# Preparing three output tiles inside the attention stage, in memory that the pooled weights leave

## The chip, the core and the metric

The kernel runs on one core of one Trainium2 chip. The core has a matrix engine (TensorE, in the profile PE, its weight loads PEld), a vector engine (DVE), a scalar engine (ACT), a general engine (POOL) and a queue that issues most transfers (SP). The metric is device microseconds of one execution; a time is the median of several executions.

## The reference

A two-layer encoder trunk is applied with the same weights to two inputs: `x_prompt` (2048 tokens of 1024 numbers) and `x_sample` (512 tokens). One layer is

```
h    = rms_norm(x, pre_g)
u, zp, q, k, v, za = split(h @ w_in)                  # 1024 -> 3072
pool = pooling_mixer(u) * silu(zp)                    # 4 windows, a small map per group
q, k = rope(q), rope(k)                               # 4 heads, 2 maps each, 64 wide
o    = (softmax(q0 k0) - lam * softmax(q1 k1)) @ v    # per head, v 128 wide
attn = rms_norm(o, subln_g) * (1 - lambda_init) * silu(za)
y    = concat(pool, attn) @ w_out                     # 1024 -> 1024
x    = x + rms_norm(y, post_g)
```

All arrays are float32.

## The kernel before

Every product is made of three matrix products of numbers split in a high and a low part (fp32r), so that almost every tensor that TensorE reads has first been through `split`: a copy of the high part, mostly on ACT, and a subtraction for the low part, on DVE or POOL. PSUM has eight banks of 128 x 512: four called `sc`, two `tr`, one `ot`, one `mm`. A name's banks are used in turn, so a new user of a bank waits for the last reader of its old contents.

**Order.** The instructions of PE, ACT, DVE and POOL run in the order in which the Python code issues them (`manual_schedule`). SP is not in that set: its transfers are put in order by the compiler's own schedule, by when their data and memory are expected to be free. Memory is taken from two stacks of pools, one growing from the left and one from the right; a pool that is opened where a closed one lay makes each of its tiles wait for the old tiles under it.

**Attention** (`attention`). Work comes in blocks of one head and 256 queries. A block of the prompt has four lots, a block of the sample has one; a lot is four score tiles of 128 x 512. In one pass of the loop, called a step here, PE computes the scores of a lot (L441, L442), ACT takes the exponentials of the lot before (L468), DVE the maxima of the present one (L452, L448), PE turns two units of older probabilities by transposes (`flip`, L493) into a `tr` bank, which ACT and DVE split (L110, L115), and multiplies units by the values (`values`, L510). The score of a lot goes into the `sc` bank that the exponential of the lot before has to read first. When a block's exponentials are done, POOL joins its two maps (`combine`, L474 to L484); only then can the block be turned. `finish` and `scales` (L515 to L550) square the result, multiply by `sg` and the gate, store it to `mh` in DRAM (L521) and compute each token's and head's scale, kept in `rstat`.

**The filler.** TensorE has other work to fill each step with: `fill` takes six matmuls per step, first of the input projections that are left and then of `pooled_outputs` (L699), the pooled half of the output projection, whose results go through bank `mm` and tile `yo` to `ys` in DRAM. The weights of this half lie in pool `wop` (eight tiles of 4 KB per partition), those of the attention half in `woa`. With them lie, on the right, `yo`, `mixp` (pooled inputs) and `kv` (keys and values of the sample) in the stack `aux`, and one raw weight row `wor` in `kept`.

**The end of attention.** The last block of the prompt's head 3 is followed by the last one of the sample. When the latter's lot is made, `mix_ahead` asks for the first 256 tokens of `mh` in the `wor` tile (L1088). Once no lot is left, each step also takes ten pieces of `first_outputs` (L1091): for the first two token tiles (128 tokens each), `spread` puts each token's scale into a row by four transposes (L744, into a `tr` bank), `rescale` multiplies (L748, DVE) and splits (ACT high, POOL low, tile `mixp`), and then come the 48 matmuls (L754) of the two tiles with the attention half of `w_out`, into the four `sc` banks.

In what follows the steps of the end are named by what PE does in them. Step A holds the last prompt lot, step B the sample's last lot, step C no lot and the last six matmuls of the pooled outputs; D to H turn the last prompt block and the last sample block, two units each, and the attention ends after H.

**The output stage** (`phase3`). For each of the 20 token tiles: load `y` (the pooled half) and `mixh` (the attention output, for two tiles at once); `scale`, that is `spread` and `rescale`, two tiles ahead; 24 matmuls (`products`); `y = ps + y` on DVE (L800); then `post`: square sum on ACT (L839), its power on POOL (L843), product on DVE (L845), sum with the residual `xr` on POOL (L847), store. Its pools `y`, `d`, `m` are opened on the left after attention's. In layer 0 the next layer's pools (86 KB) are opened below them, and from the thirteenth tile on `nxt.prepare` adds the norms and transposes (L172, L177, in `tr` banks) of layer 1.

## Time and profile before

| | us |
|---|---|
| median of 3 runs | 3176.3 (3175.72 to 3178.85) |
| the profiled execution | 3172.6 |
| its span | 3170.6 |
| PE busy | 3070.9 |
| DVE, ACT, POOL busy | 2057.8, 1719.0, 1773.2 |

The profiled execution lies 3.7 us below the median, and 2.0 us of it lie outside the span. A line of a timeline gives start, duration, engine, source line, operation and how often, and in brackets the idle time before it and what ended it. A line of the waits gives the sum, the count and the longest of one kind of wait. A table of stretches gives, for each, its length, the busy time of each engine with instructions in brackets, the clock that TensorE was granted (1.00 is full) and the DMA share. The profile says 0.99 for the clock over the whole span.

### The profile page before, as it was taken

The numbers are of one execution on the slowest core, as the hardware profiler recorded it, in microseconds if no ns is written. First come the engines' busy times: TensorE is split into PE (matmuls) and PEld (weight loads), VectorE is DVE, ScalarE is ACT, GpSimd is POOL, SyncE is SP. The second block draws the span as 40 slices with busy tenths as digits, with TensorE's granted clock in tenths as the row PEclk, the third lists the DMA queues.
The fourth block names the chain that finished last, engine by engine and source line by source line (L and its number), as shares of the span: only waits on it lengthen the run. The fifth ranks groups of instructions, "written<-read, shape, count | busy, mean of one in ns | idle before, by whom it ended". The sixth has DMA issues, their size and how long they took to land. (4 is left out here: it accounts for less than half of the span.)

```text
span 3170.6 us, 48480 instructions
## 1 busy us (share of the span) xinstructions
PE 3070.9 (97%) x17016; PEld 2590.7 (82%) x17016; DVE 2057.8 (65%) x3249; ACT 1719.0 (54%) x3915; POOL 1773.2 (56%) x1978
## 2 busy tenths in 40 slices
PE   8999999999999999998999999999999999999888
PEld 6898888778887888886778888887788878888776
DVE  3354255688888887774634543556888988777644
ACT  3244233377777777772332442333777777777622
POOL 1000122289997888885710001122999978888846
PEclk9999999999999999998999999999999999999999
DMA  5354357643424334435854544577434243353367
GB/s 200 117 159 148 125 159 206 205 139 94 130 67 137 104 107 141 125 98 194 317 174 120 157 140 132 171 200 222 117 91 124 64 140 114 97 152 114 91 212 260
DMA packets 298900, 464.54 MB, mean 147 GB/s; under 512 B 26144, under 2 KB 180768, under 8 KB 298656
## 3 DMA queue, kind: packets, MB, share of 16 engines
q1 hardware_dynamic: 292032, 439.42, 46.3%
q10 hardware_dynamic: 6624, 22.02, 1.8%
q8 instruction: 134, 2.20, 0.3%
q14 instruction: 110, 0.90, 0.1%
HBM read 293.57 MB, written 167.77 MB: 146 GB/s over the span
## 5 line engine op out<-in xcount | busy, mean ns | idle before, releaser
L452 DVE TENSOR_REDUCE mx<-sc 128x1 f32<-128x512 f32 x1024 | 649.9, 683 | 184.8 <-PE sc L442 184.6
L468 ACT ACTIVATE e<-sc,nm 128x512 f32<-128x512 f32 x1088 | 732.4, 694 | 32.0 <-DVE nm L455 28.4
L484 POOL TENSOR_TENSOR e<-e,e 128x1024 f32<-128x1024 f32 (+1 forms) x288 | 666.5, 2314 | 24.0
L278 PE MATMUL sc<-hth,wh 128*128 128x512 f32 x1408 | 555.7, 395 | 0.0
L278 PE MATMUL sc<-htl,wh 128*128 128x512 f32 x1408 | 554.4, 394 | 0.0
L278 PE MATMUL sc<-hth,wl 128*128 128x512 f32 x1408 | 552.7, 393 | 0.7 <-DVE ss L166 0.7
L110 ACT ACTIVATE ath<-tr 128x512 fp32r<-128x512 f32 x544 | 329.2, 606 | 259.6 <-PE ot L510 190.4
L441 PE MATMUL sc<-ks,q 128*128 128x512 f32 x1024 | 434.8, 425 | 3.4 <-ACT e L468 3.4
L442 PE MATMUL sc<-ks,q 128*128 128x512 f32 x1024 | 406.1, 397 | 0.0
L115 DVE TENSOR_TENSOR atl<-tr,ath 128x512 fp32r<-128x512 f32 x544 | 364.7, 682 | 53.4 <-ACT ath L110 53.3
L510 PE MATMUL ot<-ath,v 128*128 128x256 f32 x2176 | 368.1, 291 | 7.7 <-DVE mt L520 7.7
L493 PEld LDWEIGHTS tr<-ident,e 128*128 128x128 f32 x2176 | 267.3, 141 | 91.5 <-DVE atl L115 22.4
L493 PE MATMUL tr<-ident,e 128*128 128x128 f32 x2176 | 329.6, 275 | 11.8 <-DVE atl L115 9.9
L483 POOL TENSOR_SCALAR e<-e,nco 128x1024 f32<-128x1024 f32 (+1 forms) x288 | 327.8, 1138 | 15.0
L510 PEld LDWEIGHTS ot<-ath,v 128*128 128x128 f32 x2176 | 309.4, 189 | 32.0 <-DVE mt L520 11.1
L168 POOL TENSOR_TENSOR rs<-ss,mhalf 128x1 f32<-128x1 f32 x40 | 25.5, 638 | 554.0 <-DVE ss L166 554.0
L278 PEld LDWEIGHTS sc<-hth,wl 128*128 128x128 f32 x1408 | 264.6, 188 | 60.2 <-DVE wl L115 1.2
L278 PEld LDWEIGHTS sc<-hth,wh 128*128 128x128 f32 x1408 | 264.7, 188 | 58.5 <-POOL wl L115 0.3
L278 PEld LDWEIGHTS sc<-htl,wh 128*128 128x128 f32 x1408 | 264.7, 188 | 57.5 <-DVE htl L115 0.4
L441 PEld LDWEIGHTS sc<-ks,q 128*128 128x128 f32 x1024 | 194.3, 190 | 65.1 <-ACT e L468 38.7
L115 DVE TENSOR_TENSOR wl<-wr,wh 128x1024 fp32r<-128x1024 f32 x94 | 121.3, 1293 | 183.5 <-ACT wh L110 182.0
L468 ACT ACTIVATION_READ_ACCUMULATOR e<-sc,nm 128x1 f32 x1088 | 231.6, 213 | 0.0
(151 smaller groups left out, 5729.5 us busy)
## 6 DMA issues: line engine op xcount, KB each, us to landing
wr<-in_w_in SPq DMA_DIRECT2D x128, 512.0 KB, 4.2
q<-qs_p SPq DMA_DIRECT2D x128, 256.0 KB, 4.1
ks_p<-hl SPq DMA_DIRECT2D x64, 256.0 KB, 3.3
vs_p<-hl SPq DMA_DIRECT2D x128, 128.0 KB, 2.6
qs_p<-hl SPq DMA_DIRECT2D x64, 256.0 KB, 3.5
mp_p<-hl SPq DMA_DIRECT2D x32, 512.0 KB, 3.7
ks<-ks_p SPq DMA_DIRECT2D x64, 256.0 KB, 5.8
v<-vs_p SPq DMA_DIRECT2D x32, 512.0 KB, 6.1
```

Of the source, the lines that this page charges most:

```text
L110: nc.scalar.activation(hi, src, AF.Copy)
L115: lo_eng.tensor_tensor(lo, src, f32(hi), op=ALU.subtract)
L168: nc.gpsimd.tensor_tensor(rs, ss, mhalf[:, :1], op=ALU.pow)
L278: nc.tensor.matmul(ps, lhsT=w[k // 4][m][:, k % 4, ns], rhs=h[:, k, :], start=k + i == 0, stop=k == KT - 1 and i == 2)
L441: nc.tensor.matmul(ps, lhsT=q[:, m, 0, ts], rhs=kk, start=True, stop=False)
L442: nc.tensor.matmul(ps, lhsT=q[:, m, 1, ts], rhs=kk, start=False, stop=True)
L452: nc.vector.reduce_max(s["mx"][:, ch : ch + 1], s["ps"][ch], axis=AX.X)
L468: nc.scalar.activation(dst, s["ps"][ch], AF.Exp, bias=s["nm"], accum_out=s["b"]["z"][s["qt"]][:, m, ch : ch + 1])
L483: nc.gpsimd.tensor_scalar(x1[:, :n], x1[:, :n], nco, 0.0, op0=ALU.mult, op1=ALU.add)
L484: nc.gpsimd.tensor_tensor(x0[:, :n], x0[:, :n], x1[:, :n], op=ALU.add)
L493: nc.tensor.transpose(ps[:, j, qt * P : (qt + 1) * P], e[kt // 8][:, kt % 8 * P : (kt % 8 + 1) * P], ident)
L510: nc.tensor.matmul(b["ot"][:, :QB], lhsT=b["vs"][v][kt // 8][:, kt % 8, :], rhs=at[:, j, :], start=unit + i == 0, stop=kt == nkt - 1 and i ...
```

## The change

`first_outputs` is rewritten, and the memory around it rearranged.

- The first tile is scaled and split one step earlier: when the sample's last lot is made, at the end of step A, `fill.first(1)` runs its `spread` and `rescale`. The product goes to a `yo` tile, the parts to the raw weight tile on the left.
- The rest waits until the filler is empty: `fill_first` returns as long as pooled products or their tails are left. Then `aux` is closed, that is `wop`, `yo` and `mixp`, and the output stage's pools `d` and `m` are opened in that memory. The next 256 tokens of `mh` are asked for, tile 1 is scaled and split, tile 0 multiplied, tile 2 scaled and split, tile 1 multiplied.
- In these three the low parts are subtracted on DVE, not on POOL. In the output stage POOL does it as before.
- `phase3` takes `d` and `m` as they are, with tile 2 ready. Its `spread` writes bank `mm` (the filler's) instead of a `tr` bank. The `scale` of tile 2 there ends at once.
- `kv` moves from `aux` to `kept`, which now stays open to the end of the stage.
- In the last layer a tile of 72 KB is opened below pool `y` and never used, so that `y` lies where attention's `q`, `k`, `e1` and `raw` lay instead of `e0` and `v`.

```diff
+PAD = 18 * 1024
...
+                        if qb == nq - 1:
+                            fill.first(1)
                         yield from block(sa, n // ns, n % ns, *skv)
...
-    def rescale(ps, src, m, hl):
+    def rescale(ps, src, m, hl, lo_eng):
         nc.vector.tensor_tensor(m, ps.rearrange("p (h n) -> p h n", h=H), src, op=ALU.mult)
-        split(hl[:, 0], hl[:, 1], m, nc.scalar, nc.gpsimd)
+        split(hl[:, 0], hl[:, 1], m, nc.scalar, lo_eng)
...
-    def phase3(l, wo, scaling, pairs, early, kept, es, nxt):
+    def phase3(l, wo, scaling, pairs, early, ready, ph, mixed, kept, es, nxt):
+        if not nxt:
+            es.enter_context(sbuf("pad", 1)).tile([P, PAD], F32, name="pad")
         y_p = es.enter_context(sbuf("y", 6))
-        mixed = ExitStack()
-        d_p = mixed.enter_context(sbuf("d", 3))
-        m_p = mixed.enter_context(sbuf("m", 3))
+        d_p, m_p = ph["d"], ph["m"]
...
-            ps = bank("tr")
+            ps = bank("mm")
             spread(ps, s["st"], s["t"])
...
-        for s in tiles[:3]:
+        for s in tiles[:2]:
             for _ in scale(s):
                 pass
...
-            if 3 <= n + 2 < len(order):
+            if n + 2 < len(order):
                 scaling.append(scale(tiles[n + 2]))
-            if n == 2:
-                kept.close()
...
         mixed.close()
+        kept.close()
...
-                po.update(open_pools(kept, "right", wor=1))
-                po.update(open_pools(aux, "right", wop=1, yo=2, mixp=2, kv=1))
+                po.update(open_pools(kept, "right", wor=1, kv=1))
+                po.update(open_pools(aux, "right", wop=1, yo=2, mixp=2))
...
             def first_outputs():
-                split_tiles = []
-                for t in range(2):
+                def prepare(t, m, hl):
                     ps = bank("tr")
                     spread(ps, pr, t)
+                    rescale(ps, pairs["p", t // 2 * 2 * P][:, :, t % 2 * P : (t % 2 + 1) * P], m, hl, nc.vector)
+                    ready["p", t] = hl
                     yield
-                    m = po["yo"].tile([P, TB], F32, name="yo").rearrange("p (h n) -> p h n", h=H)
-                    hl = po["mixp"].tile([P, 2, H, P], F32R, name="mixp")
-                    rescale(ps, pairs["p", 0][:, :, t * P : (t + 1) * P], m, hl)
-                    split_tiles.append(hl)
-                    yield
-                for t, hl in enumerate(split_tiles):
+                def multiply(t):
                     early["p", t] = []
                     for ns in halves:
                         ps = bank("sc")
                         early["p", t].append(ps)
-                        for i, _ in enumerate(head_products(ps, hl, wo, ns)):
+                        for _ in head_products(ps, ready["p", t], wo, ns):
                             yield
+                m = po["yo"].tile([P, TB], F32, name="yo").rearrange("p (h n) -> p h n", h=H)
+                yield from prepare(0, m, pa["raw"].tile([P, 2, H, P], F32R, name="wor"))
+                aux.close()
+                ph["d"] = mixed.enter_context(sbuf("d", 3, "right"))
+                ph["m"] = mixed.enter_context(sbuf("m", 3, "right"))
+                pairs["p", 2 * P] = ph["d"].tile([P, H, 2 * P], F32, name="mixh")
+                nc.sync.dma_start(pairs["p", 2 * P], pr["mh"][:, :, 2 * P : 4 * P])
+                for t in range(2):
+                    yield from prepare(t + 1, ph["m"].tile([P, H, P], F32, name="mixs"), ph["m"].tile([P, 2, H, P], F32R, name="hl"))
+                    yield from multiply(t)
...
             def fill_first(n):
+                if n > 2 and (products or tails or fresh):
+                    return
                 for _ in range(n):
                     next(first, None)
```

## The prediction

> **What bounds the kernel now.** First the page: one engine is busy nearly all the time, so the question is only what PE waits for, where the change works.

> ```profile
> span 3170.6 us, 48480 instructions
> ## 1 busy us (share of the span) xinstructions
> PE 3070.9 (97%) x17016; PEld 2590.7 (82%) x17016; DVE 2057.8 (65%) x3249; ACT 1719.0 (54%) x3915; POOL 1773.2 (56%) x1978
> ```

> Then PE's waits from step B to the first tiles of the output stage, in layer 0 (1416 to 1476 us) and layer 1 (2993 to 3053 us, its three longest):

> ```profile
> PE sc L754 <- POOL mixp L115: 7.4, 1, 7.4
> PE sc L754 <- DVE y L800: 5.9, 1, 5.9
> PE sc L754 <- ACT mixp L110: 1.0, 1, 1.0
> PE tr L532 <- DVE shl L115: 0.9, 1, 0.9
> PE tr L532 <- ACT shl L110: 0.7, 1, 0.7
> PE ot L510 <- DVE mt L520: 0.5, 1, 0.5
> ```

> ```profile
> PE sc L754 <- POOL mixp L115: 7.4, 1, 7.4
> PE sc L754 <- ACT hl L110: 6.9, 1, 6.9
> PE sc L754 <- ACT mixp L110: 1.0, 1, 1.0
> ```

> Two holes in each layer: one in step C, where the early products wait for their low parts, and one where the output stage begins. They cost more than the wait: afterwards PE runs at a lower granted clock. The table of stretches, begun where PE takes up work after each hole, shows it (length, busy time and instructions of PE, PEld, DVE, ACT and POOL, granted clock, DMA share, GB/s):

> ```profile
> 1433.87:1437.49 3.62, 3.62 (x14) 3.04 (x14) 0.00 (x0) 0.80 (x2) 1.18 (x1) 0.53 0.19 72
> 1469.10:1475.02 5.92, 5.92 (x16) 4.66 (x17) 2.43 (x4) 2.93 (x5) 1.81 (x3) 0.52 1.04 399
> 3011.14:3014.60 3.46, 3.46 (x13) 2.87 (x14) 0.00 (x0) 0.73 (x2) 1.18 (x1) 0.56 0.54 173
> 3047.26:3053.15 5.89, 5.33 (x16) 3.91 (x17) 2.34 (x4) 2.93 (x5) 2.29 (x2) 0.62 1.04 388
> 1554.32:1557.60 3.28, 3.28 (x16) 2.56 (x16) 3.27 (x3) 2.44 (x6) 3.28 (x2) 1.00 0.67 184
> 1563.41:1567.36 3.95, 3.95 (x12) 3.29 (x13) 2.48 (x4) 2.06 (x3) 3.23 (x4) 0.55 0.68 188
> ```

> Length times (1 - clock) is the loss: 3.62 x 0.47 = 1.7, 5.92 x 0.48 = 2.8, 3.46 x 0.44 = 1.5, 5.89 x 0.38 = 2.2. So the holes cost 1.0 + 7.4 + 1.7 + 5.9 + 2.8 = 18.8 us in layer 0 and 1.0 + 7.4 + 1.5 + 6.9 + 2.2 = 19.0 in layer 1. Why the first is so long shows on POOL in layer 0:

> ```profile
> 1417.47 0.47 POOL L477 TENSOR_TENSOR zc<-zc 128x4 f32<-128x4 f32 x2 [2.81 <-ACT e L468]
> ...
> 1420.30 2.40 POOL L484 TENSOR_TENSOR e<-e,e 128x1024 f32<-128x1024 f32 x1
> ```

> The low parts (L115) are issued to the same queue behind the joining of the last prompt block and of the sample's. Yet the prompt's first half of keys is joined at 1422.7, and only that is needed for PE's next transposes.

> **The change part by part.** *Removed.* Step C no longer scales, splits and multiplies; PE goes straight to step D. The work itself (two spreads, 48 products) is only moved, and a third spread comes forward from the output stage: PE's sum of work is the same. Gone are the waits of 1.0 and 7.4 and the slow clock behind them: 10.1 in layer 0, 9.9 in layer 1. The ten products per step, held back by one step, now also lie in step G (ten instead of two), ahead of the values that waited 0.5 for `mt`: that goes too, in each layer.

> *Tile 0 ahead of step B.* Its input is there: the transfer into `wor` was issued early, since SP's order is not the program's.

> ```profile
> L1088 SPq DMA_DIRECT2D wor<-mh_p x2: 534/534/535, 1246.1 to 2823.4; - x2
> ```

> But its high part stands in ACT's queue ahead of the exponentials of the last prompt lot, and the scores of step B reuse the banks that these read. Before, ACT began them at 1414.61 and PE the scores at 1416.26:

> ```profile
> 1414.61 0.68 ACT L468 ACTIVATE e<-sc,nm 128x512 f32<-128x512 f32 x1
> ```
> ```profile
> 1416.26 0.40 PE L441 MATMUL sc<-k,q 128*128 128x512 f32 x1
> ...
> 1423.88 1.03 PE L744 MATMUL tr<-ident,rstat_p 128*128 128x128 f32 x8
> ```
> ```profile
> L110 ACT ACTIVATE ath<-tr 128x512 fp32r<-128x512 f32 x544 | 329.2, 606 | 259.6 <-PE ot L510 190.4
> ...
> L115 DVE TENSOR_TENSOR atl<-tr,ath 128x512 fp32r<-128x512 f32 x544 | 364.7, 682 | 53.4 <-ACT ath L110 53.3
> ```

> Now: spread 0.6 from 1416.26, product 0.68, copy 0.61, so the first exponential starts at 1418.2 (3.6 later than before) and ends at 1418.9. PE, free at 1416.6 after its four transposes, waits 2.3; with the later banks I take 2.4 per layer. The ends are 0 and the whole 3.6. The joining on POOL moves by the same 3.6: it starts at 1421.1, and the first half is ready 5.2 later (as from 1417.47 to 1422.7), at 1426.3. PE, which came to its spreads of step C at 1423.88, comes to the transposes of step D 0.4 + 2.4 later than that, at 1426.7. That it still has to wait for POOL is just avoided, by 0.4 us.

> *Tile 1 in step D.* Its spread follows both groups of transposes and takes the bank of the first, which ACT and DVE must first split: 0.61 + 0.68 = 1.3 us of new wait per layer (0 to 2). Tile 2, in step E or F, stands behind values and five products and waits for nothing; its `mixh` is asked for three steps ahead. The two subtractions of the tail on DVE have two inputs in SBUF. The nearest such instruction beside a working POOL is this:

> ```profile
> L845 DVE SCALAR_TENSOR_TENSOR y<-y,ry,gpost x39: 1268/1285/2317, 1476.8 to 3158.6; 128x1024 f32<-128x1024 f32 x39
> ```

> It takes 1.3, at worst 2.3. Only tile 1's subtraction falls into POOL's joining (of the sample); I take half of that extra 1.0, rounded up to 0.6, per layer, with 0 and 1.3 as ends. [...]

> *The output stage's start.* Tile 2 is ready, so the 6.9 for `hl` in layer 1 goes. In layer 0 the hole was DVE's sum, whose `y` came late:

> ```profile
> 1461.18 0.33 SPq L521 DMA_DIRECT2D mh_s<-mt  x1
> 1461.56 0.43 SPq L764 DMA_DIRECT2D gpost<-in_post_norm_g  x1
> 1462.05 2.43 SPq L771 DMA_DIRECT2D y<-ys_p  x4
> ```

> The `y` loads stood in SP's queue behind the last store of attention. I read the queue as placing them when all the memory under pool `y` is free: before, that included `kv` and `mixp` (layer 0) and `e0` (layer 1), used to the end. After it, in both layers the last user is tile 0's `hl` in the raw tile, done in step E, some 15 us earlier, while the DMA engines are nearly idle. So `y` is there. What is late next is DVE: after the last scales (two instructions of 256 columns, about 0.5 each) comes the sum that frees a bank, 0.68: 1.7 us of wait, near the hole of 2.1 in the 1554 row after which the clock stayed at 1.00, so no slow clock. The pad, `kv`'s move and `kept`'s later end add no instruction.

> *Bank `mm`.* In layer 0, while the next norm is prepared, PE waits for DVE, which lags with the rescaling:

> ```profile
> PE tr L177 <- DVE mixs L748: 7.8, 2, 5.7
> ```
> ```profile
> 1545.33 0.60 PE L744 MATMUL tr<-ident,rstat_s 128*128 128x128 f32 x4
> ...
> 1551.59 0.60 PE L744 MATMUL tr<-ident,rstat_s 128*128 128x128 f32 x4
> ...
> 1554.32 0.66 PE L177 MATMUL tr<-ident,xt 128*128 128x128 f32 x4 [2.13 <-DVE mixs L748]
> ```
> ```profile
> 1562.59 0.68 DVE L748 TENSOR_TENSOR mixs<-tr,mixh 128x512 f32<-128x512 f32 x1
> ```

> With the spreads in a bank of their own the transposes L177 wait no more, but each spread waits for the rescaling of the tile before: the one at 1551.59 until 1554.3 (2.7), the next, due at about 1561.4 (a tile's 6.3, from 1545.33 to 1551.59, and two groups of transposes later), until 1563.3 (1.9). That is 4.6 instead of 7.8 + 3.95 x 0.45 = 9.6. As DVE is the slow one there, part comes back later: I take 2 of the 5, with 0 and 9.6 as ends.

> **The sum.** Gone: 10.1 + 0.5 + 5.9 + 2.8 = 19.3 in layer 0, 9.9 + 0.5 + 6.9 + 2.2 = 19.5 in layer 1, together 38.8. New: 2 x (2.4 + 1.3 + 0.6 + 1.7) = 12.0. Bank `mm`: 2. Net 28.8, call it 29. The profiled execution of 3172.6 (3170.6 of span and 2.0 around it) becomes 3143.6; it lies 3.7 below the median, so the median of 3176.3 becomes 3147.

> **The rivals.** *Loads still late.* If SP's queue keeps `y` behind the last store, both starts keep about 8.7 (5.9 + 2.8) instead of 1.7: 14 us less, 3161. For it: it was so in both layers. Against: the memory is free earlier.

> *The clock falls in the new gaps.* If the 2.4 before step B and the row of 0.7, 0.9 and 1.7 at the end each bring the slow clock, they cost 1.5 to 2.8 each: 2 x (1.5 + 2.8) = 8.6, 3156. Against it stands the stretch at 1554 with 1.00; for it, that several gaps fall close together. [...] No row here shows it for gaps under 5 us.

> *The change doesn't do what it says.* If the filler is not empty in step D, `fill_first` keeps returning and the products come after attention, where they cover nothing. Then each of the five steps D to H waits for its own splits, 1.3 to 2.6: 6.5 to 13 per layer, out of a gain of 14; about 3168. Against it: the filler takes six per step and two steps per half tile, and ended in step C.

> *Slower: one bank for the spreads.* A spread now cannot start before the rescaling of the tile before has ended; from 1551.59 to 1563.3 that took 11.7. Should all eight last tiles of layer 0 get this pace (12.1 with the spread) instead of 6.3, they cost 8 x 5.8 = 46 less the 9.6 lost there now, 37: with the other 27 of the forecast slower by 10, 3186. It decides from a lag of about 11 us in each of them. Against it: 11.7 is one tile's.

> **How the numbers follow.** Forecast 0.68, late loads 0.11, clock 0.10, filler 0.07, slower 0.04. The forecast's own ends: 9 us to each side (step B -4.8 to +2.4, `mm` -7.6 to +2, the subtraction 1.3 each way, not all together): 3138 to 3156. Taking in clock and late loads, 3138 to 3162. About 0.2% (6.4 us) is what can be told from no change: faster than 3169.9 are the first three and most of the filler case, 0.93; same 0.03; slower 0.04.

> **What would show it.** In the new profile: step C followed by transposes L493 without POOL's wait; in step B a wait of scores L441 for ACT of 2 to 3 us; in step D a spread L744 waiting about 1.3 for DVE; SP's first `y` loads ahead of the last `mh` stores; PE clock near 1 through the end of attention; in layer 0 waits of L744 for `mixs` in place of those of L177. I am wrong if the first L754 of tile 2 waits more than 3 us, or if a slow clock follows step B.

## The result, and the profile after

The changed kernel takes 3150.7 us (median of 10 runs, 3146.4 to 3169.4). The kernel before, run beside it, takes 3179.9 (10 runs, 3175.7 to 3182.9). The two medians lie 29.2 us apart, where 29 were forecast. The ratio by which the experiments below are compared is 0.9919, with a 95% interval of 0.9901 to 0.9936: 25.8 us faster by it, from 20 to 31. The profiled executions lie 21.5 us apart (spans of 3170.6 and 3149.1). In this document a line number of the changed kernel is that of the kernel before plus 1 (the scores, turns and splits), plus 3 (the spreads L747, products L757 and sums L803).

The head of the page of the changed kernel: PE's busy time has fallen by 5.5 us, in part because fewer matmuls run at the low clock (mean granted clock 0.990 before, 0.994 now; the median 128x512 product of L754 took 0.39 to 0.40 us before, and those from 1433.8 to 1437.2 us, at 0.50, took 0.63 to 0.80), and the rest of the 21.5 is idle time that went:

```profile
span 3149.1 us, 48450 instructions
## 1 busy us (share of the span) xinstructions
PE 3065.4 (97%) x17016; PEld 2585.4 (82%) x17016; DVE 2069.5 (66%) x3255; ACT 1719.1 (55%) x3915; POOL 1768.4 (56%) x1972
```

PE's waits of the changed kernel from step B to the first tiles of the output stage, in layer 0 (1416 to 1476 us; sum, count, longest). Layer 1 (2985 to 3040 us) gives the same six rows:

```profile
PE sc L442 <- DVE wor L116: 2.1, 1, 2.1
PE sc L757 <- DVE y L803: 1.6, 1, 1.6
PE tr L494 <- DVE sq L541: 1.4, 2, 1.2
PE tr L747 <- DVE atl L116: 1.0, 1, 1.0
PE tr L533 <- DVE shl L116: 0.9, 1, 0.9
PE tr L533 <- ACT shl L111: 0.7, 1, 0.7
```

The 7.4 for POOL, the 1.0 for ACT, the 5.9 and the 6.9 are gone, and nothing waits for POOL. The table of stretches of the changed kernel, first behind the wait of step B, then behind that of step D, then behind the start of the output stage in layers 0 and 1 (the seventh column is the granted clock):

```profile
1420.63:1428.54 7.91, 7.91 (x47) 6.61 (x48) 4.45 (x9) 6.91 (x20) 5.43 (x7) 1.00 0.21 68
1430.60:1435.72 5.12, 3.93 (x23) 3.32 (x24) 4.36 (x5) 0.64 (x2) 4.83 (x6) 1.00 0.96 293
1459.92:1463.00 3.08, 3.08 (x8) 2.39 (x9) 1.74 (x3) 2.30 (x4) 1.04 (x3) 0.50 0.97 313
3026.12:3029.20 3.08, 3.08 (x10) 2.44 (x11) 1.74 (x3) 2.30 (x4) 1.04 (x3) 0.57 0.08 32
```

The clock holds behind 2.1 and 1.0, and does not behind the row of 0.7, 0.9 and 1.6 at the end: 3.08 x 0.50 = 1.5 us lost in layer 0, 3.08 x 0.43 = 1.3 in layer 1. SP's queue shows the `y` loads of layer 0 ahead of the last stores of `mh`, not behind them:

```profile
1433.23 11.34 SPq L774 DMA_DIRECT2D y<-ys_p  x4
...
1452.98 0.32 SPq L522 DMA_DIRECT2D mh_p<-mt  x1
```

Both kernels have 17016 matmuls, and outside the attention's end in the same order. So the first one of a stretch can be found in both by counting, and a stretch be measured from its first matmul to that of the next. In us:

| stretch | before | changed | difference | forecast |
|---|---|---|---|---|
| start of the pooled outputs, layer 0 (from 977 us) | 36.6 | 38.8 | +2.2 | 0 |
| end of attention and first three tiles of the output stage, layer 0 | 123.4 | 111.7 | -11.7 | -13.3 |
| rest of the output stage and start of layer 1 | 125.1 | 123.1 | -1.9 | -2 |
| start of the pooled outputs, layer 1 | 34.2 | 36.9 | +2.7 | 0 |
| end of attention and output stage, layer 1 | 214.6 | 200.6 | -14.0 | -13.5 |
| behind the last matmul | 12.8 | 14.7 | +1.9 | 0 |
| all the rest | 2623.9 | 2623.1 | -0.8 | 0 |

The two rows that the change was about come to -25.7 of the forecast -26.8. What is missing stands in rows that the prediction costed at nothing. The experiments ask three things: which part of the change did it, whether the waits that are left are what the prediction said, and where the 2.2 and 2.7 come from.

### The profile page after: what moved, and what is told of

Same layout as the page of the kernel before. It is cut to its first block, busy times and chain, and to the rows that moved or that the text cites. A ratio compares the mean times of both kernels' runs of the same rounds, so it can differ in the third digit from the quotient of the medians.

```text
span 3149.1 us, 48450 instructions
## 1 busy us (share of the span) xinstructions
PE 3065.4 (97%) x17016; PEld 2585.4 (82%) x17016; DVE 2069.5 (66%) x3255; ACT 1719.1 (55%) x3915; POOL 1768.4 (56%) x1972
## 5 line engine op out<-in xcount | busy, mean ns | idle before, releaser
L442 PE MATMUL sc<-ks,q 128*128 128x512 f32 x1024 | 433.9, 424 | 3.3 <-ACT e L469 3.1
L116 DVE TENSOR_TENSOR atl<-tr,ath 128x512 fp32r<-128x512 f32 x544 | 364.9, 682 | 25.7 <-ACT ath L111 25.5
L494 PE MATMUL tr<-ident,e 128*128 128x128 f32 x2176 | 328.7, 274 | 18.1 <-DVE atl L116 14.6
L484 POOL TENSOR_SCALAR e<-e,nco 128x1024 f32<-128x1024 f32 (+1 forms) x288 | 329.9, 1145 | 14.9
L442 PEld LDWEIGHTS sc<-ks,q 128*128 128x128 f32 x1024 | 193.8, 189 | 64.7 <-ACT e L469 38.3
```

The costliest lines, as they stand in the source:

```text
L116: lo_eng.tensor_tensor(lo, src, f32(hi), op=ALU.subtract)
L442: nc.tensor.matmul(ps, lhsT=q[:, m, 0, ts], rhs=kk, start=True, stop=False)
L484: nc.gpsimd.tensor_scalar(x1[:, :n], x1[:, :n], nco, 0.0, op0=ALU.mult, op1=ALU.add)
L494: nc.tensor.transpose(ps[:, j, qt * P : (qt + 1) * P], e[kt // 8][:, kt % 8 * P : (kt % 8 + 1) * P], ident)
```

## The experiments

Each kernel was timed against the kernel before on the same chip. The kernel before took 3177.3 to 3181.4 us in the five series (medians), so a row's ratio says more than its median. An interval of 0.15% is 5 us wide to each side, so what is smaller is read from the stretches of the profile (in us, as above: pooled start of layers 0 and 1; attention's end with the first tiles in layer 0; the rest of the output stage with layer 1's start; attention's end with the output stage in layer 1; the tail).

| kernel | median (runs) | ratio, 95% interval | pooled 0 | pooled 1 | end 0 | rest 0 | end 1 | tail |
|---|---|---|---|---|---|---|---|---|
| before | 3179.9 (10) | 1 | 36.6 | 34.2 | 123.4 | 125.1 | 214.6 | 12.8 |
| changed | 3150.7 (10) | 0.9919 [0.9901, 0.9936] | 38.8 | 36.9 | 111.7 | 123.1 | 200.6 | 14.7 |
| low parts on DVE alone | 3165.7 (5) | 0.9955 [0.9942, 0.9967] | 36.6 | 34.1 | 114.2 | 129.2 | 206.6 | 12.5 |
| `kv` moved alone | 3176.3 (11) | 0.9992 [0.9981, 1.0004] | 39.0 | 37.0 | 120.7 | 126.6 | 216.1 | 12.6 |
| low parts back on POOL | 3148.4 (6) | 0.9901 [0.9874, 0.9927] | 36.6 | 35.3 | 112.6 | 121.9 | 200.0 | 14.8 |
| bank undone | 3153.3 (6) | 0.9927 [0.9910, 0.9943] | 37.7 | 33.0 | 111.4 | 125.0 | 202.0 | 15.2 |
| no pad | 3150.7 (4) | 0.9912 [0.9898, 0.9925] | 40.7 | 35.4 | 111.4 | 122.7 | 200.2 | 14.8 |
| tile 0 later | 3150.3 (6) | 0.9921 [0.9906, 0.9935] | 36.6 | 35.4 | 112.8 | 122.0 | 201.0 | 14.8 |
| tile 0's high part on DVE | 3147.9 (6) | 0.9907 [0.9878, 0.9936] | 39.0 | 35.3 | 109.8 | 122.1 | 198.0 | 14.8 |
| half of tile 2 in `ot` | 3149.5 (4) | 0.9908 [0.9893, 0.9923] | 39.1 | 34.0 | 111.6 | 123.4 | 199.5 | 14.8 |
| two banks for spreads | 3148.1 (5) | 0.9900 [0.9873, 0.9927] | 37.9 | 35.4 | 110.1 | 124.5 | 197.4 | 16.7 |
| pooled weights' low parts on POOL | 3161.7 (11) | 0.9952 [0.9933, 0.9970] | 41.9 | 39.1 | 111.6 | 123.3 | 203.8 | 14.7 |
| three mendings together | 3142.1 (4) | 0.9887 [0.9871, 0.9902] | 39.1 | 34.0 | 105.6 | 125.2 | 194.2 | 16.8 |
| those, pooled low parts last | 3140.4 (6) | 0.9900 [0.9863, 0.9936] | 36.4 | 33.2 | 107.0 | 124.3 | 195.2 | 16.2 |

### One part alone: the low parts on DVE

To the kernel before:

```
-        split(hl[:, 0], hl[:, 1], m, nc.scalar, nc.gpsimd)
+        split(hl[:, 0], hl[:, 1], m, nc.scalar, lo_eng)      # nc.vector for the two tiles of step C
```

> The kernel before, with one part of the change alone: the low parts of the two tiles in step C made on DVE instead of POOL; steps, memory and banks stay as before. Theory (the 7.4 us were the wait behind POOL's joining, and either way out of it would do): in step C PE waits some 2.5 us for high and low parts instead of 1.0 and 7.4, the slow clock behind it goes, the start of the output stage keeps its holes; 7.6 us less per layer, 15 in all, 3163 against 3178 (ratio 0.9953). Rival (DVE's subtraction has two inputs in SBUF and runs beside POOL's joining, which holds it as it held the pooled weights' low parts, 2.1 us each time): PE waits 4 to 5 us in step C and the slow clock stays; 8 us less, 3170 (0.9975).

3165.7 us, ratio 0.9955: the theory. PE's waits in step C of layer 0 (1400 to 1500 us):

```profile
PE sc L754 <- ACT mixp L110: 1.0, 1, 1.0
PE sc L754 <- DVE mixp L115: 0.6, 1, 0.6
```

The 7.4 for POOL has become 0.6 for DVE. The holes at the start of the output stage stay (5.7 and 7.2 in its two layers). By the ratios that is 0.45% of the change's 0.81%, 14 of 26 us: about half could be had by naming another engine in one call. In its profile the two ends are 9.2 and 8.0 us shorter, and the rest of layer 0 is 4.1 longer; 3.6 of that is that PE ran more of it at a granted clock of 0.50 (from 1546.08 to 1552.90 and from 1556.32 to 1563.14).

### The other way round: the steps of the change, the low parts on POOL

```
-   rescale(ps, ..., m, hl, nc.vector)
+   rescale(ps, ..., m, hl, nc.gpsimd)
```

> The changed kernel, with the low parts of the three tiles back on POOL, as the kernel before had them; the steps stay. It asks which of the two did it: the other engine, or the later step. Theory (the 7.4 us came from products issued right behind a low part that stood behind POOL's joining; now tile 1's products come 10 us after its spread): the low part of tile 1 ends at about 1439.6 in layer 0 behind the sample's joining and is wanted at 1443.9, so nothing waits for it; DVE loses an instruction that POOL held (1.65 us), and PE's wait at the transposes behind the squares goes from 1.2 to 0.3. Some 1.8 us less in all, 3148.9 (ratio 0.9913). Rival (the engine did it): PE waits 3 us or more for POOL at tile 1's first products in each layer, 3157 (0.994).

3148.4 us: no slower than the changed kernel, and no wait for POOL in any of the steps. Its waits in layer 0 at step B and behind the squares:

```profile
PE sc L442 <- ACT e L469: 2.1, 1, 2.1
PE tr L747 <- DVE atl L116: 1.8, 1, 1.8
PE tr L494 <- DVE sq L541: 0.5, 2, 0.3
```

The 1.4 behind the squares has fallen to 0.5, as expected, though in layer 0 the spread of step D waits 0.8 longer. Hence the engine did not matter once the steps had changed: a low part that is wanted 10 us later may stand behind POOL's joining. Either half of the change removes the 7.4, and the two don't add up.

### The bank of the spreads undone

```
-            ps = bank("mm")
+            ps = bank("tr")          # in the output stage's scale()
```

> The changed kernel, with the spreads of the output stage back in the bank of the transposes: the bank alone is undone. Theory (the bank saves 4.2 us in the output stage of layer 0, but ACT's chain of last norms and stores gains less than PE, so that layer 1 gives 2.6 back): the transposes L178 wait 7.8 us again for the rescaling, the waits for the weights' parts at layer 1's start (0.97 and 0.53 us) and the slow clock there are gone; net 1.6 us longer, about 3152.3 (ratio 0.9924). Rival A (the bank is worth all it removes): nothing comes back, 3155. Rival B (the gain in the stage is not the bank's, but that tile 2 is ready): no change, 3150.7, and L178 does not wait.

3153.3 us. In the profile the rest of layer 0's output stage with layer 1's start is 1.9 us longer (125.0 against 123.1); expected were 1.6. PE's waits at the last tiles of layer 0 in this kernel (1530 to 1570 us), and then the same in the changed one:

```profile
PE tr L178 <- DVE mixs L751: 5.1, 2, 3.0
```
```profile
PE mm L747 <- DVE mixs L751: 4.0, 3, 2.1
```

The transposes wait again for the rescaling (5.1, not the 7.8 of before), which in the changed kernel only the spreads do. And at layer 1's start of the changed kernel (1580 to 1600 us) there are waits that the kernel with the bank undone does not have:

```profile
PE sc L279 <- ACT wh L111: 1.0, 1, 1.0
PE sc L279 <- DVE wl L116: 0.5, 1, 0.5
```

What follows: the bank's gain is taken back where the next layer begins. There ACT makes the weights' high parts behind its last store, which waits for POOL's last sum:

```profile
1583.76 5.02 ACTq L853 DMA_DIRECT2D xs_s<-y  x2
1588.84 1.06 ACT L166 ACTIVATE junk<-xt 128x1024 bf16<-128x1024 f32 x1 [5.74 <-POOL y L850]
1589.80 0.19 ACT L166 ACTIVATION_READ_ACCUMULATOR junk<-xt 128x1 f32 x1
1589.89 1.04 ACT L111 ACTIVATE wh<-wr 128x1024 fp32r<-128x1024 f32 x1
```

By counting matmuls, layer 1's start alone (the last 80 of the stretch) took 18.1 us before and 20.7 in the changed kernel; with the bank undone it takes 18.3. Of those 2.6 us, 1.7 are lost to the clock, which was 0.50 from 1592.95 to 1596.37. So the 2 us net that the prediction left of the bank's 5 come out, but not for its reason: it had put the loss down to DVE in the output stage.

### The pad taken away

```
-        if not nxt:
-            es.enter_context(sbuf("pad", 1)).tile([P, PAD], F32, name="pad")
```

> The changed kernel without the pad that shifts the output stage's pool in layer 1. Theory (a load waits for the last user of the memory under its tile, and the loads behind it on SP's queue wait with it): without the pad the first y of layer 1 lies in memory that attention still uses, so its loads are issued behind the last store of attention (3022.9 in the changed kernel's trace, where they now come at 2999.4); PE's wait for DVE's sum at layer 1's start is some 4 us longer than the 1.6 now, and the slow clock adds 1 to 2: 5 to 6 us more, 3156 (ratio 0.9936). Rival (the pad does nothing, since another pool's end has already freed that memory): the loads come as early as now, 3150.7.

The theory fell in its price. The loads do come late again in layer 1 (3018.79 instead of 2999.44), but the start waits exactly as long (the sum of `y` has line L801 here):

```profile
3018.36 0.33 SPq L522 DMA_DIRECT2D mh_p<-mt  x1
3018.79 0.86 SPq L772 DMA_DIRECT2D y<-ys_p  x2
3022.07 0.32 SPq L522 DMA_DIRECT2D mh_s<-mt  x1
```
```profile
PE sc L757 <- DVE y L801: 1.6, 1, 1.6
```

Two `y` get in ahead of the very last store, and that is enough for the first sums. The median is that of the changed kernel, so in layer 1 the pad buys nothing that can be measured. The case of layer 0, where all four loads stood behind the last store, was not undone by itself.

### Tile 0 one step later

```
-                        if qb == nq - 1:
-                            fill.first(1)
                         yield from block(sa, n // ns, n % ns, *skv)
+                        if qb == nq - 1:
+                            fill.first(1)
```

> The changed kernel, with tile 0 of the prompt prepared one step later (behind the sample's scores instead of ahead of them). Theory (the high part on ACT holds up the exponentials, and step B's scores their banks): PE's wait of 2.1 us at the scores L442 goes in both layers and nothing takes its place, since tile 0 is wanted only in step D; the attention's end is 4.2 us shorter in all, and the time about 3146.5 against 3150.7 for the changed kernel (ratio to the kernel before 0.9906 instead of 0.9919). Rival (the wait only moves): the high part then stands ahead of the sample's exponentials, POOL joins the sample 2 us later, and the transposes or the spread of step D wait 2 us for it; the time stays at 3150.7.

3150.3 us: the rival. The wait of step B is gone, and a longer one stands at the spread of step D, in layer 0 3.5 instead of 1.0. PE, then ACT in this kernel:

```profile
1429.10 0.65 PE L747 MATMUL tr<-ident,rstat_p 128*128 128x128 f32 x4 [3.45 <-DVE atl L116]
```
```profile
1423.45 0.63 ACT L111 ACTIVATE wor<-yo 128x512 fp32r<-128x512 f32 x1 [2.37 <-DVE yo L751]
...
1427.69 0.63 ACT L111 ACTIVATE ath<-tr 128x512 fp32r<-128x512 f32 x1
```

ACT stands 2.37 us idle before the high part, then come the sample's exponentials, and behind them the split for which the spread's bank waits. So it is ACT's queue that pays wherever tile 0's high part stands in it. That suggested the next kernel.

### Tile 0's high part on DVE

```
-   split(hl[:, 0], hl[:, 1], m, nc.scalar, lo_eng)
+   split(hl[:, 0], hl[:, 1], m, hi_eng, lo_eng)     # for tile 0: both nc.vector
```

> The changed kernel, with the high part of tile 0 made on DVE instead of ACT; its place ahead of step B stays. Theory (ACT's queue is what holds up step B: there the high part stands ahead of four exponentials, and in the run with tile 0 one step later it stood ahead of the sample's and PE waited 3.5 us at the next spread): ACT's exponentials start about 3 us earlier, PE's wait of 2.1 us at the scores L442 goes in both layers and does not come back at the spread of step D (1.0 to 1.8 us there as now); 4.2 us less in all, about 3146.5 (ratio 0.9906). Rival (DVE is the next to hold it: product, high part and low part stand ahead of the peaks of step B): the sample's exponentials come no earlier, the wait moves to the transposes or the spread of step D, and the time stays at 3150.7 (0.9919).

The waits of step B are gone in both layers and did not move: the spread of step D still waits 1.0 (a wait of 0.5 for `mt` is back). The ends of attention are 1.9 and 2.6 us shorter than in the changed kernel, 4.5 against the 4.2 expected; median 3147.9, which alone could not be told from the changed kernel's. (The span of its profiled execution, 3156.2, has 12 us more in the first part of layer 0, where its instructions are those of the others.) The trace of the changed kernel named DVE's `wor` as what ended the wait because that was the last of several semaphores; ACT's queue was the cause, as the prediction had it.

### A bank for the start of the output stage

```
-                    ps = bank("sc")
+                    ps = bank("ot" if s is tiles[2] and nh == 0 else "sc")
```

> The changed kernel, with the first half of tile 2's products in the bank of the attention's output, which is free by then, instead of a bank that the sum of tile 0 must first empty. Theory (the three waits of 0.7, 0.9 and 1.6 us are one hole for the clock, and the last one is DVE's sum): the 1.6 goes in both layers, the next half waits for nothing, because DVE's sum ends while PE multiplies for 2.7 us; without the long one the slow clock behind it (3.08 us at 0.50, 1.5 us lost) goes too: 3.1 us per layer, 6.3 in all, time about 3144.5 (ratio 0.9899). Rival (the two short waits alone bring the slow clock): only the 1.6 goes, 3.3 us in all, 3147.4 (0.9909). Second rival (DVE stays behind): the wait returns at the second half, 3150.7.

3149.5 us: by the time alone the second rival. The profile says more. The 1.6 is gone, and in this execution the same short waits of 0.7 and 0.9 leave the clock alone, as the theory has it (the last section shows one where they don't); the stretches of this kernel that answer to those of 0.50 and 0.57:

```profile
1461.38:1464.46 3.08, 3.08 (x17) 2.56 (x17) 2.78 (x6) 0.71 (x1) 2.69 (x9) 1.00 1.05 234
3025.00:3028.08 3.08, 3.08 (x17) 2.55 (x17) 2.77 (x6) 0.70 (x1) 2.70 (x9) 1.00 0.66 171
```

From the last squares to the fourth spread it takes 13.6 us (1461.16 to 1474.74) where the changed kernel takes 16.7 (1457.90 to 1474.59): 3.1. Then a later spread waits 1.8 for a rescaling, in both layers, and takes more than half of that back; in layer 0 another 1.7 went to the clock behind step B (last section). So the second rival has part of the truth, with another place: DVE is behind, but it is the spreads' single bank that shows it.

### Two banks for the spreads

The kernel above, and in `scale`:

```
-            ps = bank("mm")
+            ps = bank("mm" if s["t"] % 2 else "ot")
```

> The changed kernel, with tile 2's first half in the bank of the attention's output and the spreads of the output stage in that bank and the filler's by turns. Theory (the 1.6 us at the start and the later waits of spreads for the rescaling, 1.8 us at the start of both layers and 4.3 in layer 0 before the next layer, are all waits for a bank): 3.1 us per layer go at the start and the 1.8 do not come back; the 4.3 in layer 0 go, but layer 1 then waits that much longer for its weights' parts. 6.3 us less in all, 3144.5 (ratio 0.9899). Rival (DVE is behind anyway, and the bank only decides where PE waits for it): the 1.8 come back as a wait of products for the sum of y, and the time is that of the run with tile 2's half alone, 3149.5 (0.991).

3148.1 us. In layer 1 the end and the output stage are 3.2 us shorter (197.4), but 2.0 of it come back in the tail; in layer 0 PE now waits 2.4 for a sum of `y` and 3.1 for transposed inputs (1455 to 1570 us) where it waited for the bank:

```profile
PE tr L178 <- DVE htl L116: 3.1, 2, 2.1
PE sc L757 <- DVE y L803: 2.4, 1, 2.4
```

In layer 0 the rival is right for the last tiles: DVE is the slow one there, and the bank only decides where PE waits.

### `kv` moved alone

To the kernel before:

```
-   po.update(open_pools(kept, "right", wor=1))
-   po.update(open_pools(aux, "right", wop=1, yo=2, mixp=2, kv=1))
+   po.update(open_pools(kept, "right", wor=1, kv=1))
+   po.update(open_pools(aux, "right", wop=1, yo=2, mixp=2))
```

> The kernel before, with the move of the sample's keys and values alone (kept instead of aux, so that the pooled weights lie 8 KB lower); the instructions are the same. Theory (the 2.2 and 2.7 us lost at the start of the pooled outputs are a matter of phase: DVE's fourth low part of the pooled weights started 0.09 and 0.06 us behind POOL's joining and was held for 2.1 us): the move itself costs nothing, 3179.9 (ratio 1.0000, within 0.001); where that low part starts ahead of POOL's joining it takes 1.2 to 1.6 us, where it starts behind, 3.4. Rival (the new places or the changed order of transfers cost it): 4.9 us longer, 3184.8 (1.0015), with the fourth low part at 3.4 us in both layers.

Ratio 0.9992 [0.9981, 1.0004]: the move costs nothing that can be measured. Yet this profile has the long pooled starts, 39.0 and 37.0. The fourth low part on DVE and the joining on POOL beside it, in layer 0: the kernel before, the changed one, the one with `kv` moved.

```profile
1003.38 1.59 DVE L115 TENSOR_TENSOR wol<-wor,woh 128x1024 fp32r<-128x1024 f32 x1
```
```profile
1003.99 3.25 POOL L484 TENSOR_TENSOR e<-e,e 128x1024 f32<-128x1024 f32 x1
```
```profile
1003.24 3.38 DVE L116 TENSOR_TENSOR wol<-wor,woh 128x1024 fp32r<-128x1024 f32 x1
```
```profile
1003.15 2.38 POOL L485 TENSOR_TENSOR e<-e,e 128x1024 f32<-128x1024 f32 x1
```
```profile
1005.33 3.41 DVE L115 TENSOR_TENSOR wol<-wor,woh 128x1024 fp32r<-128x1024 f32 x1
```
```profile
1005.26 2.39 POOL L484 TENSOR_TENSOR e<-e,e 128x1024 f32<-128x1024 f32 x1
```

Whoever starts first is done in nearly its own time, and the other one takes 0.8 to 2.2 us longer. In the twelve profiles in which DVE makes this part ahead of the step's second split, there are 24 such pairs. In 13 POOL came 0.05 to 0.09 us first and DVE took 3.38 to 3.42; in 11 POOL came 0.20 to 0.62 us later, DVE took 1.22 to 1.61 and POOL 3.24 to 3.27 instead of 2.4. Both kinds occur with `kv` moved (tile 0 later has one of each, the undone bank two of the second) and among the nine kernels whose code there is that of the changed one. The sums of the two pooled starts are 70.7 to 76.0 in the three kernels whose attention is that of before, and 70.7 to 76.1 in the nine that share it with the changed kernel; the two profiles compared here drew 70.8 and 75.7. So 4.9 us, by which the spans lie closer together than they otherwise would, are the luck of these two executions, and the theory of phase holds. (No kernel was profiled twice: that it is luck is read from kernels that are alike in this stretch.)

### The pooled weights' low parts on POOL

```
-                split(wo["h", k], wo["l", k], raw, nc.scalar, nc.vector)
+                split(wo["h", k], wo["l", k], raw, nc.scalar, nc.gpsimd)
```

> The changed kernel, with the low parts of the four pooled weights' rows made on POOL instead of DVE. Theory (the start of the pooled outputs, 36.6 to 39.0 us in layer 0 and 33.0 to 37.0 in layer 1 in six profiles, is a matter of whether DVE's low part or POOL's joining comes first): four instructions of some 2.6 us on POOL, in gaps of 2 to 3.8 us in which it waits for exponentials; DVE has no more instruction of 3.4 us, its work in that stretch falls by 1.2 to 3.4 us in each of four steps, and PE's waits for DVE there (2.1, 2.4 and 2.3 us) shrink. Both stretches come to about 33 us: 9 to 10 us less than in the changed kernel's profile, about 3141 to 3144 (ratio 0.989 to 0.990). Rival (POOL has no such gaps: the joining comes 2.6 us later and the transposes wait for it in each of the four steps): 5 to 10 us more, 3158 (0.9943).

3161.7 us, the rival's side, but by a road that neither had. PE's longest wait there, and SP's queue at that time:

```profile
PE sc L442 <- DMA ks<-ks_p: 5.3, 1, 5.3
```
```profile
1004.88 0.34 SPq L677 DMA_DIRECT2D wor<-in_w_out  x1
1005.31 1.08 SPq L421 DMA_DIRECT2D ks<-ks_p  x2
```

The third low part stands on POOL behind a joining. The weight row that it reads comes free later, the next row's load therefore waits at the head of SP's queue (until 1004.88; 999.57 in the changed kernel), and the keys of the next head stand behind it.

### The mendings together

Three mendings: tile 0's high part on DVE, the low parts of the tiles on POOL, and the banks (half of tile 2 in `ot`, spreads in two banks).

> The changed kernel with what the runs so far bore out, together: tile 0's high part on DVE, the low parts of the three tiles on POOL, tile 2's first half in the bank of the attention's output and the spreads in that bank and the filler's by turns. Theory (these waits are separate): the 2.1 us at step B go in both layers (4.2), the 1.2 at the squares' transposes (1.8 in all, of which the first part alone took some already), and 3 us come from the banks; 8 to 9 us less, about 3142 (ratio 0.9890). Rival (they are the same slack, and what is won in one place is waited for in the next): no better than the best of the three alone, 3148 (0.9905).

3142.1 us, ratio 0.9887 [0.9871, 0.9902]: the theory, and better than both kernels that this study compares. PE's waits in layer 1 (2970 to 3060 us), all that is left of the holes:

```profile
PE tr L747 <- DVE atl L116: 1.0, 1, 1.0
PE tr L533 <- DVE shl L116: 0.9, 1, 0.9
PE ot L747 <- DVE y L803: 0.7, 1, 0.7
PE tr L533 <- ACT shl L111: 0.7, 1, 0.7
PE tr L494 <- DVE sq L541: 0.5, 2, 0.3
```

The two ends are 6.1 and 6.4 us shorter than in the changed kernel. In each, 4 us of that is idle time of PE and 1.7 is that the clock stayed at 1.00, which the next kernel, with the same waits at the end of layer 1, did not get. Of the gain, 2.1 come back in layer 0's rest and 2.1 in the tail.

### The pooled weights' low parts behind the second split

The kernel with the mendings, and the low part with the next row's load put off until the step's second split is issued:

```
+                held.append(rest)      # low part on DVE, then load_rows of the row after next
...
                 flip_split(late[2])
                 flipped.append(late)
+            fill.after()               # runs what is held
```

> The kernel with the three mendings together, and one more: the low parts of the four pooled weights' rows stay on DVE but come behind the second split of the step and behind the output's product (and the load of the next row with them), instead of ahead of both. In ten profiles in which DVE makes them ahead, the two stretches at the start of the pooled outputs took 36.6 to 40.7 and 33.0 to 37.0 us (39.1 and 34.0 in the kernel with the three mendings), and DVE's fourth low part took 3.4 us where POOL's joining had begun 0.05 to 0.09 us before it. Theory (a held low part costs because the split that PE waits for stands behind it): PE's waits of 2.1 and 2.4 us, and of 2.3 where it is held, go or shrink to under 1 us, whoever comes first; the stretches fall to about 34 and 32 us, 7 us in all, and the time to 3135 (ratio 0.9866). Rival (the peaks of the next step now stand behind it, and ACT's exponentials behind those, or keys on SP's queue come late as with POOL): the waits come back as PE's waits for ACT or a transfer, and the time stays at 3142 or rises.

3140.4 us (six runs, 3139.0 to 3176.5), ratio 0.9900 [0.9863, 0.9936], not to be told from 3142.1. The profile shows half of the theory: the two pooled starts take 36.4 and 33.2, 3.5 less than with the mendings alone. But only 1.2 of that is idle time of PE; the rest is that one stretch at a clock of 0.50 falls there instead of three. The low parts are held here too (2.86 and 2.73 us for two of the four in layer 0), but the 2.3 behind the fourth is gone and the 2.4 for `mt` has fallen to 1.1 (in layer 0). The 2.1 at the first transposes stayed, since it was never theirs: a rotation on DVE (L299 before) took 2.81 us there beside POOL's joining in the kernel before as well. And a wait of 1.7 has come at the values. So the held low part cost 2.3 us where it came up, and it can be moved off the path.

## Why the prediction was right, point by point

- **What goes.** The waits of 1.0 and 7.4 with the slow clock behind them, the 0.5 for `mt`, and the 5.9 and 6.9 are gone, as the sum had it. Of the slow clock behind the last two (2.8 and 2.2 us), 1.5 and 1.3 came back. The cause given for the 7.4, products wanted at once behind POOL's joining, is borne out from both sides: with the low parts on DVE alone it shrank to 0.6, and with the later step alone it vanished.
- **Step B.** 2.4 forecast, 2.1 measured, by way of ACT's queue; both kernels that took the high part out of ACT's way there removed the wait.
- **Step D.** 1.3 for the spread forecast, 1.0 measured. PE came to the transposes without a wait: POOL had joined the first half at 1427.9 and they began at 1428.5, 0.6 us to spare where 0.4 had been worked out.
- **The subtraction of tile 1.** 0.6 forecast, with 0 and 1.3 as ends. It took 1.65 us, tile 2's 0.69, and the wait behind the squares rose from 0.3 to 1.2, by 0.9. POOL's joining of 1.28 us began 0.18 before it. So the subtraction took 0.96 us longer than tile 2's, most of the 1.1 us that POOL's instruction still had to run, and the 0.9 lies between the forecast's 0.6 and its end of 1.3, about a whole joining.
- **The start of the output stage.** 1.7 forecast, 1.6 measured, DVE's sum behind the last scales. But the sentence "so no slow clock" failed: 1.5 and 1.3 us were lost behind it. That is half of the rival on the clock, which priced the end of attention at 2.8. It had named the reason, several gaps close together: 2.64 and 2.51 us without work of PE fell into the one stretch of 3.41 us ahead of the slow one in layers 0 and 1 (1456.42 to 1459.83 and 3023.14 to 3026.55). That step B's wait brought none in this profile was luck, worth 1.7 us each time: of 14 such waits in seven profiles five did (last section). And that no row shows it for gaps under 5 us was true of the rows quoted, not of the trace: at the pooled start of the kernel before, the clock was 0.50 for 3.4 us from 993.51 on, behind a wait of 2.4 us.
- **Bank `mm`.** 4.6 left of 9.6 and 3 of the 5 given back later was the working; 1.9 us net were measured for 2 forecast, and undoing the bank cost 1.9. The waits came to 4.0, but a slow clock that the working had as gone stayed behind one of them (0.50 from 1545.17 to 1548.58, 1.7 us), and the time given back was lost at the start of layer 1, in ACT's queue and to the clock, not to DVE. The 2 was a guess, and that it fits is luck.
- **"The pad, `kv`'s move and `kept`'s later end add no instruction."** Costed at nothing, and rightly. The 4.9 us that the profile shows at the pooled starts are not the move's, as the run with `kv` moved alone shows.
- **The reason given for the early loads** holds in the trace, but its weight was overrated in layer 1: loads in the old order did no harm there. The rival with late loads, at 14 us, took for granted that all of them would stand behind the last store.
- **Not seen at all:** the tail. In layer 1 the chain of post-norms on ACT, POOL and DVE sets the end, and PE's gain of 14.0 lost 1.9 to it.

The new waits come to 2 x (2.1 + 1.0 + 0.9 + 1.6) = 11.2 us, for 12.0 forecast, and the slow clock behind them to 2.8, where nothing was forecast. So the mechanism holds term by term but for the bank's, and the main term left out is the clock. Of the forecast 29 the two profiles show 21.5, the ratio 25.8 and the medians 29.2. These differ by 8 us among themselves, and the luck at the pooled starts alone is 4.9; that the medians meet the forecast to a fraction of a microsecond is luck as well.

## What to carry to other kernels

A wait that goes by way of a queue has two cures, another engine or a later use; try the cheaper one by itself before rearranging memory: here the two did not add up. Where PE is made faster at one place, look for the next thing that paces it: here the following layer's ACT chain and the post-norms gave back 2 us each. Before explaining a few microseconds between two profiles, measure the same stretch in several profiles of code that is the same there: here it varied by 5 us.

## What the runs showed of the hardware

Two engines beside each other. In the 24 pairs of a DVE subtraction (`wol`, 128x1024) and POOL's sum of two tiles (`e`, 128x1024) one always held up the other: DVE took 3.4 instead of 1.2 us, or POOL 3.25 instead of 2.4, according to which of the two started first. It was unexpected that in an unchanged piece of code the winner changes from profile to profile, with 2.3 us on PE at stake.

```profile
1418.87:1422.29 3.42, 1.66 (x9) 1.39 (x10) 1.76 (x3) 3.01 (x8) 0.00 (x0) 1.00 0.00 0
1422.29:1425.70 3.41, 3.41 (x20) 2.72 (x20) 3.20 (x6) 2.41 (x7) 2.60 (x6) 1.00 0.21 77
```
```profile
1420.22:1423.64 3.42, 1.31 (x10) 0.93 (x9) 1.68 (x3) 2.41 (x6) 0.00 (x0) 1.00 0.00 0
1423.64:1427.05 3.41, 3.41 (x12) 2.73 (x12) 2.51 (x5) 1.87 (x6) 2.08 (x5) 0.50 0.21 77
```

This is a reason why the column of the first end varies where the waits are the same. Over all 14 traces, without the first 60 and the last 20 us, 84 stretches at full clock had more than 1.95 us idle, and all 84 were followed by one at 0.50. Of 58 with 1.50 to 1.95, 20 were; of the more than 12000 with less, none. The 2.4 us for `mt` lie between: the fullest stretch had 1.89 us idle before and 1.88 after, with 0.50 behind it in the one (993.51) and 1.00 in the other. The row of 0.7, 0.9 and 1.6 us slowed the clock in all 14 cases. Without the 1.6 it happened in two of eight; here is one, the end of layer 1 in the kernel with the pooled low parts last, whose waits are 0.69 and 0.87:

```profile
3011.11:3014.53 3.42, 1.86 (x10) 1.28 (x9) 2.25 (x6) 0.80 (x2) 1.34 (x5) 1.00 0.91 314
3014.53:3017.94 3.41, 3.41 (x12) 2.72 (x11) 3.16 (x6) 1.92 (x3) 1.87 (x6) 0.50 0.28 112
```

No run set the offset of this grid on purpose; it differed by itself, while the wait stayed the same.
